# A weight sum of a Strassen pair as one vector instruction instead of two

## The chip, the cores and the metric

One Trainium2 chip, one core. The metric is device time in microseconds of one whole execution, all stages from the first load to the last store. The engines are called as in the profile: PE is the matrix engine and PEld its weight loads, DVE the vector engine, ACT the scalar engine, POOL the general-purpose engine, and SP the engine whose queue issues most of the DMAs.

## What is computed

A two-layer trunk for a prompt group of 512 tokens and a sample group of 8 tokens that share all weights. Everything is f32. In words, for each layer:

```python
h = rmsnorm(x, norm_g)
b_c, c_c, x_c, g_c, q, k, v, g_r = split(h @ w_in)        # w_in: 2048 x 8192
y_conv = b_c * conv3(c_c * x_c) * silu(g_c)               # causal, depthwise, width 3
y_ret = groupnorm(retention(rope(q), rope(k), v)) * gn_g * silu(g_r)
x = x + concat(y_conv, y_ret) @ w_out                     # 2048 x 2048
x = x + sigmoid(x @ w_pg) * (p[i] @ w_ple)                # 2048 x 2048, 256 x 2048
```

A last RMSNorm gives the outputs, and the convolution rows and retention states of both groups are outputs too.

## The kernel before

The 512 + 8 = 520 tokens lie along the free dimension, feature tiles of 128 along the partitions. An activation tile is 128x520, and it is used in two halves of 260 tokens, `LEFT` and `RIGHT`. A matmul multiplies a 128x128 weight tile with a 128x260 half.

Exactness comes from splitting each f32 operand into a rounded part `hi` and a remainder `lo` (both fp32r); `mm3` then does three matmuls, hi·hi, hi·lo and lo·hi, at lines 247, 248 and 249. So each weight tile, after its DMA, is rounded by ACT (line 229) and its remainder is formed by DVE (line 230) before PE can use it. `split_w` does both, for up to four K tiles (128x512) at once.

The large products take the output columns two tiles at a time; such a pair is one call of `pair`. If its row number `s` is 0, it is done directly (`plain`). Otherwise its first `s` K tiles go through one level of a Strassen scheme with seven products instead of eight (`strassen`), and the K tiles from `s` on are done directly at its end. With `q = s // 2`, a pair loads four weight blocks of `q` K tiles, `w11`, `w21`, `w22` and `w12`, and forms four weight sums in place with `add`. Most pairs have `s` of 14 or 16, so `q` is 7 or 8; one has `s` = 12 and three have `s` = 8. There are 84 pairs with `s` > 0 in the program.

```python
w11 = raws(src0, 0)
times(a, w11, k1, True, False)                 # product 1: no sum
w21, w22 = raws(src1, 0), raws(src1, q)
add(w11, w11, w21, SUB)
add(w21, w21, w22, ADD)
times(b, w21, t1, True, False)                 # product 2: after two sums
add(w21, w22, w11, SUB)
times(a, w21, t2, False, True)                 # product 3: after a third sum
w12 = raws(src0, q)
add(w21, w12, w21, SUB)
times(d, w12, ...); times(a, w11, t3, ...)     # products 4 and 5
times(b, w21, ...)                             # product 6: after the fourth sum
times(a, w22, t4, False, True)                 # product 7
```

`add` (its instruction is line 319), `times` and `raws` each cut their `q` K tiles into parts of at most `CHA`, `CHS` and `CHL` tiles, all four before. The raw weights lie in a ring of 32 K tiles (`raw_ring`), which is exactly four blocks of eight; the split weights lie in a ring of 60 K tiles (`split_ring`), where a part of four takes eight, four of `hi` and four of `lo`. A part of the split ring comes free when PE has read it.

The order on each engine isn't the order of the code. A scheduler with a model of the engines lays out the instructions of all engines when the program is built; sums and splits are raised in priority by `WPRIO`. Each engine then works strictly in the order that is written. The copies of PSUM banks, which PE waits for, are at line 307 on ACT and DVE.

The program goes through each layer in stages: the heads (q, k, v and gate of four retention heads), the convolution (16 pairs, `CONVS`), the output projection (`OUT_ROWS`) and the gate projection (`GATES`).

Of the kernel before, what the change touches and what calls it, by code (L numbers as in the profile page):

```python
# [29 lines left out]
NSLOT = 75  # L30
CH = 4
CHS = 4
CHA = 4
CHL = 4
CK = 256
BUSY = 10**9
# [155 lines left out]
def trunk_kernel(  # L192
# [40 lines left out]
    def chunks(a, b, most=CH):  # L233

        n = (b - a + most - 1) // most
        e = [a + (b - a) * i // n for i in range(n + 1)] if n else [a]
        return list(zip(e, e[1:]))
# [52 lines left out]
    def strassen(x, src0, src1, s, step=None):  # L290
# [24 lines left out]
        def add(out, x, y, op):  # L315
            for i, j in chunks(0, q, CHA):
                n = slice(P * i, P * j)
                with tc.high_priority(offset=WPRIO):
                    V.tensor_tensor(out[:, n], x[:, n], y[:, n], op)  # L319
# [1159 lines left out]
```

## Time and profile before

| | |
|---|---|
| median of 3 runs | 2168.1 us (2167.59 to 2169.01) |
| the profiled execution, first to last instruction (its span) | 2167.3 us |
| PE busy | 2147.8 us, 17861 matmuls |
| DVE busy | 1896.1 us, 3849 instructions |
| ACT busy | 1264.5 us, 2647 instructions |
| DMA | 387.31 MB, mean 179 GB/s |

The span is the profiled execution's own time; the median of the runs is 0.8 us above it. Busy is the time in which an engine has an instruction at work. An instruction's duration in the trace reaches to the end of its writes, and the next one on the same engine may start a little earlier, so durations of a group add up to more than its share of the busy time.

### The profile page before, as it was taken

To read this page: it belongs to the slowest core of one execution; us is meant where nothing else is said; L and a number is where in the kernel's file an instruction comes from. 1 tells how busy PE (TensorE), PEld (TensorE's weight loads), DVE (VectorE), ACT (ScalarE), POOL (GpSimd) and SP (SyncE) were. 2 spreads that over 40 slices of the span, in tenths; PEclk is the share of its full clock that TensorE was granted. 3 is DMA by queue.
4 is the path that set the end of the run, shared out by engine and by line. 5 is a ranking of instruction groups with operands and counts; after the bars stand their busy time and mean duration, and the time that the engine had idled before them with its cause. 6 is when DMAs were issued, how large, how long until landed. Compare 5 with 4: busy or idle time off the path is not lost. (4 is left out here: it accounts for less than half of the span.)

```text
span 2167.3 us, 48178 instructions
## 1 busy us (share of the span) xinstructions
PE 2147.8 (99%) x17861; PEld 2142.1 (99%) x17861; DVE 1896.1 (87%) x3849; ACT 1264.5 (58%) x2647; POOL 430.6 (20%) x746
## 2 busy tenths in 40 slices
PE   9999999999999999999999999999999999999998
PEld 9999999999999999999999999999999999999998
DVE  8889988998999987987997988989999998879884
ACT  8656655565555655655765655565645555456565
POOL 2313222211001211200212222231111022011011
PEclk9999999999999999999999999999999999999999
DMA  8555565545543745645645566664464355566455
GB/s 288 171 175 197 181 217 184 178 157 175 158 129 118 238 156 187 215 154 160 215 144 175 172 213 191 189 209 170 151 182 149 120 158 202 176 207 200 128 164 198
DMA packets 182861, 387.31 MB, mean 179 GB/s; under 512 B 25888, under 2 KB 56352, under 8 KB 182624
## 3 DMA queue, kind: packets, MB, share of 16 engines
q1 hardware_dynamic: 128704, 212.98, 31.6%
q0 software_dynamic: 53056, 169.84, 23.8%
q8 instruction: 140, 2.29, 0.4%
q10 hardware_dynamic: 864, 1.39, 0.2%
q14 instruction: 97, 0.79, 0.1%
HBM read 318.96 MB, written 65.15 MB: 177 GB/s over the span
## 5 line engine op out<-in xcount | busy, mean ns | idle before, releaser
L247 PE MATMUL ps_g<-slot,split 128*128 128x260 f32 x5465 | 1531.6, 284 | 7.2 <-ACT slot L307 2.9
L248 PE MATMUL ps_g<-slot,split 128*128 128x260 f32 x5465 | 1534.3, 282 | 0.3 <-DVE slot L555 0.3
L249 PE MATMUL ps_g<-slot,split 128*128 128x260 f32 x5461 | 1519.9, 283 | 0.5 <-DVE split L230 0.5
L229 ACT ACTIVATE split<-raw 128x512 fp32r<-128x512 f32 (+2 forms) x1347 | 777.3, 596 | 583.1 <-DVE raw L319 213.2
L247 PEld LDWEIGHTS ps_g<-slot,split 128*128 128x128 f32 x5465 | 1024.0, 188 | 10.1 <-ACT slot L307 3.7
L248 PEld LDWEIGHTS ps_g<-slot,split 128*128 128x128 f32 x5465 | 1028.5, 188 | 0.5 <-DVE slot L555 0.5
L249 PEld LDWEIGHTS ps_g<-slot,split 128*128 128x128 f32 x5461 | 1019.8, 188 | 1.0 <-DVE split L230 1.0
L230 DVE TENSOR_TENSOR split<-raw,split 128x512 fp32r<-128x512 f32 (+2 forms) x1346 | 849.2, 652 | 172.5 <-PE ps_g L248 85.4
L319 DVE TENSOR_TENSOR raw<-raw 128x512 f32<-128x512 f32 (+1 forms) x660 | 428.9, 660 | 32.5 <-DMA raw<-wi 23.7
L307 ACT ACTIVATE slot<-ps_g 128x260 f32<-128x260 f32 x336 | 127.4, 381 | 140.6 <-PE ps_g L249 122.7
L551 ACT ACTIVATE slot<-slot 128x520 fp32r<-128x520 f32 (+1 forms) x212 | 109.2, 562 | 46.6 <-DVE slot L414 11.1
L552 DVE TENSOR_TENSOR slot<-slot,slot 128x520 fp32r<-128x520 f32 (+1 forms) x212 | 124.4, 620 | 4.1 <-ACT slot L551 3.9
L781 POOL DMA_DIRECT2D o_rets<-slot x64 | 35.3, 552 | 351.6 <-DVE slot L780 131.7
L307 DVE TENSOR_TENSOR slot<-ps_g,slot 128x260 f32<-128x260 f32 x168 | 70.9, 424 | 6.0 <-PE ps_g L249 3.7
L869 POOL DMA_DIRECT2D slot<-hs x64 | 46.2, 724 | 118.7 <-DVE split L230 42.7
L814 POOL DMA_DIRECT2D hs<-slot x64 | 35.6, 556 | 139.3 <-DVE slot L755 61.3
L780 DVE SCALAR_TENSOR_TENSOR slot<-slot,vs,slot 128x256 f32<-128x256 f32 x128 | 56.1, 481 | 4.5 <-ACT slot L776 4.3
L746 DVE TENSOR_TENSOR slot<-slot,slot 128x520 f32<-128x520 f32 x80 | 55.8, 698 | 4.7 <-DMA o_rets<-slot 3.7
L770 POOL DMA_DIRECT2D slot<-sret x64 | 35.5, 554 | 114.6 <-ACT split L229 37.3
L1058 POOL DMA_DIRECT2D slot<-x1s x76 | 40.8, 538 | 87.6 <-PE ps_g L249 27.2
L1209 POOL DMA_DIRECT2D x2s<-slot x30 | 16.4, 545 | 201.6 <-DVE slot L1204 200.6
L771 POOL DMA_DIRECT2D slot<-kq x64 | 34.9, 547 | 106.0 <-DVE slot L876 22.2
(217 smaller groups left out, 1733.8 us busy)
## 6 DMA issues: line engine op xcount, KB each, us to landing
raw<-wi SPq DMA_DIRECT2D x377, 256.0 KB, 3.9
raw<-wo SPq DMA_DIRECT2D x128, 256.0 KB, 5.4
raw<-wg SPq DMA_DIRECT2D x122, 256.0 KB, 4.1
raw<-wi SPq DMA_DIRECT2D x136, 192.0 KB, 4.0
slot<-x1s POOLq DMA_DIRECT2D x76, 260.0 KB, 5.1
slot<-sret POOLq DMA_DIRECT2D x64, 256.0 KB, 4.0
hs<-slot POOLq DMA_DIRECT2D x64, 256.0 KB, 4.0
slot<-hs POOLq DMA_DIRECT2D x64, 256.0 KB, 5.2
```

Source lines behind the costliest of these rows:

```text
L229: S.activation(hi, raw, AF.Copy)
L230: V.tensor_tensor(lo, raw, F(hi), SUB)
L247: PE.matmul(out, wh, xh, start=start, stop=False, skip_group_check=more)
L248: PE.matmul(out, wh, xl, start=False, stop=False, skip_group_check=more)
L249: PE.matmul(out, wl, xh, start=False, stop=stop, skip_group_check=more)
L307: fn(*args)
L319: V.tensor_tensor(out[:, n], x[:, n], y[:, n], op)
L551: keep(S.activation(hi, src[:, n], AF.Copy))
L552: V.tensor_tensor(lo, src[:, n], F(hi), SUB)
L746: V.tensor_tensor(out[:, n], v, table[:, n], MUL)
L780: keep(V.scalar_tensor_tensor(st[:, c], k, vs[:, h, e, b : b + 1], st[:, c], MUL, ADD))
L869: SIDE.dma_start(t[:, :512].rearrange("p (m n) -> p m n", m=2), src)
```

## The change

```diff
-CHA = 4
+CHA = 8
```

`CHA` is used in one place:

```python
def add(out, x, y, op):
    for i, j in chunks(0, q, CHA):
        n = slice(P * i, P * j)
        with tc.high_priority(offset=WPRIO):
            V.tensor_tensor(out[:, n], x[:, n], y[:, n], op)
```

A sum over `q` = 8 K tiles was two DVE instructions of 128x512 and is one of 128x1024; for `q` = 7 it was 128x384 and 128x512 and is 128x896; for `q` = 6 it was two of 128x384 and is one of 128x768. The three pairs with `q` = 4 had one instruction a sum and keep it. That makes 336 sum instructions where there were 660. `times` still splits in parts of four K tiles, and the loads are still in parts of four.

The program holds the same instructions on PE, ACT, POOL and SP as before, but the scheduler lays them out anew. The next rows are DVE's, in the convolution of the second layer, before; names with `slot` are activation tiles, `raw` and `split` are the two weight rings, L319 are sums, L230 remainders.

```order
L319 TENSOR_TENSOR raw<-raw 128x512 x2
L307 TENSOR_TENSOR slot_1145_21830<-ps_g,slot_1145_21830 128x260
L746 TENSOR_TENSOR slot_1149_22061<-slot_1145_21830,slot_1048_19069 128x520
L230 TENSOR_TENSOR split<-raw,split 128x512
L319 TENSOR_TENSOR raw<-raw 128x512
L230 TENSOR_TENSOR split<-raw,split 128x512
L307 TENSOR_TENSOR slot_1146_21831<-ps_g,slot_1146_21831 128x260
L780 SCALAR_TENSOR_TENSOR slot_1142_21759<-slot_1143_21760,vs,slot_1142_21759 128x256 x2
L319 TENSOR_TENSOR raw<-raw 128x512 x2
```

The last L230 of these rows is the first part of product 2. Only three half sums stand ahead of it: the first half of both sums, and the second half of the first sum. The same place with the change:

```order
L307 TENSOR_TENSOR slot_1145_21574<-ps_g,slot_1145_21574 128x260
L746 TENSOR_TENSOR slot_1149_21801<-slot_1145_21574,slot_1048_18853 128x520
L230 TENSOR_TENSOR split<-raw,split 128x512
L319 TENSOR_TENSOR raw<-raw 128x1024
L307 TENSOR_TENSOR slot_1146_21575<-ps_g,slot_1146_21575 128x260
L780 SCALAR_TENSOR_TENSOR slot_1142_21503<-slot_1143_21504,vs,slot_1142_21503 128x256 x2
L319 TENSOR_TENSOR raw<-raw 128x1024
L784 ISA slot_1143_21504,osum<-slot_1142_21503,slot_1143_21504 128x256
L784 ISA osum 128x1
L230 TENSOR_TENSOR split<-raw,split 128x512
L784 ISA slot_1143_21504,osum<-slot_1142_21503,slot_1143_21504 128x256
L784 ISA osum 128x1
L230 TENSOR_TENSOR split<-raw,split 128x512 x3
```

Both whole sums now stand ahead of product 2's first part, which is the first of the three at the end, and so do the retention updates L780 and L784 and one other remainder, which stood behind it or elsewhere.

PE's order at the same place, before. Product 2 of this pair reads `slot_741`, `slot_757`, `slot_769` and so on; product 7 of the pair before it reads `slot_743`, `slot_759`, `slot_771`.

```order
L247 MATMUL ps_g<-slot_811_14204,split 128x260
L248 MATMUL ps_g<-slot_811_14204,split 128x260
L249 MATMUL ps_g<-slot_811_14204,split 128x260
L249 MATMUL ps_g<-slot_741_13732,split 128x260
L247 MATMUL ps_g<-slot_757_13845,split 128x260
L248 MATMUL ps_g<-slot_758_13846,split 128x260
L249 MATMUL ps_g<-slot_757_13845,split 128x260
```

And with the change:

```order
L247 MATMUL ps_g<-slot_811_14048,split 128x260
L248 MATMUL ps_g<-slot_811_14048,split 128x260
L249 MATMUL ps_g<-slot_811_14048,split 128x260
L247 MATMUL ps_g<-slot_743_13580,split 128x260
L248 MATMUL ps_g<-slot_744_13581,split 128x260
L249 MATMUL ps_g<-slot_743_13580,split 128x260
L247 MATMUL ps_g<-slot_759_13693,split 128x260
L248 MATMUL ps_g<-slot_760_13694,split 128x260
L249 MATMUL ps_g<-slot_759_13693,split 128x260
```

Product 7 of the pair before is put in front: the L249 on `slot_741`, the first matmul that needs the remainder of product 2, stands 24 places further back in PE's whole order. All in all 7979 of the program's 17827 matmuls have another place, half of these by at most 9 places and nine in ten by at most 24; the rest keep theirs.

## Rows read from the trace of the kernel before

**Rows 1.** The page: span and busy time of the engines.
```profile
span 2167.3 us, 48178 instructions
...
PE 2147.8 (99%) x17861; PEld 2142.1 (99%) x17861; DVE 1896.1 (87%) x3849; ACT 1264.5 (58%) x2647; POOL 430.6 (20%) x746
```

**Rows 2.** Groups by line and shape: busy us, mean ns, idle before.
```profile
L247 PE MATMUL ps_g<-slot,split 128*128 128x260 f32 x5437 | 1523.6, 284 | 7.2 <-ACT slot L307 2.9 <-ACT ps_g L307 1.6 <-ACT split L229 1.5
...
L319 DVE TENSOR_TENSOR raw<-raw 128x512 f32<-128x512 f32 x520 | 354.1, 688 | 17.6 <-DMA raw<-wi 12.1 <-DMA raw<-wo 2.9
...
L319 DVE TENSOR_TENSOR raw<-raw 128x384 f32<-128x384 f32 x140 | 77.4, 554 | 14.9 <-DMA raw<-wi 11.6 <-DMA raw<-wg 2.8
```

**Rows 3.** Busy us by stage: stretch, length, PE, PEld, DVE, ACT, POOL; then clock, DMA.
```profile
530.00:704.00 174.00, 174.00 (x1454) 174.00 (x1454) 158.71 (x312) 93.58 (x188) 18.33 (x24) 1.00 0.44 134
704.00:1112.00 408.00, 404.68 (x3368) 403.57 (x3367) 353.44 (x683) 247.63 (x501) 73.83 (x133) 1.00 0.58 186
...
1612.00:1786.00 174.00, 173.57 (x1443) 172.74 (x1442) 161.32 (x321) 95.14 (x200) 20.17 (x28) 1.00 0.46 142
1786.00:2145.00 359.00, 356.48 (x2963) 355.60 (x2961) 291.45 (x542) 208.47 (x428) 60.32 (x113) 1.00 0.56 183
sum 2075.00, PE 2066.72 PEld 2062.95 DVE 1828.62 ACT 1206.04 POOL 409.89; mean PE 344.45 PEld 343.82 DVE 304.77 ACT 201.01 POOL 68.31
```

**Rows 4.** What PE waited for, whole span: us in total, times, longest.
```profile
PE ps_g L247 <- ACT slot L307: 2.9, 4, 1.3
PE ps_g L247 <- ACT ps_g L307: 1.6, 2, 1.2
PE ps_g L247 <- ACT split L229: 1.5, 2, 1.3
...
PE ps_g L249 <- DVE split L230: 0.5, 1, 0.5
```

**Rows 5.** What the splits waited for, whole span: us in total, times, longest.
```profile
ACT split L229 <- DVE raw L319: 213.2, 160, 4.3
...
ACT split L229 <- PE ps_g L249: 186.2, 220, 3.9
...
DVE split L230 <- PE ps_g L248: 85.4, 109, 2.2
```

**Rows 6.** The same waits in the second convolution stage, 1612 to 1786 us.
```profile
ACT split L229 <- DVE raw L319: 30.6, 21, 4.3
...
DVE split L230 <- PE ps_g L248: 0.8, 1, 0.8
```

**Rows 7.** Timeline, 1683 to 1692 us: start, us to the last one's end, instruction.
```profile
1683.16 1.41 DVE L319 TENSOR_TENSOR raw<-raw 128x512 f32<-128x512 f32 x2
1684.49 0.42 DVE L307 TENSOR_TENSOR slot<-ps_g,slot 128x260 f32<-128x260 f32 x1
...
1685.56 0.68 DVE L230 TENSOR_TENSOR split<-raw,split 128x512 fp32r<-128x512 f32 x1
1686.28 0.69 DVE L319 TENSOR_TENSOR raw<-raw 128x512 f32<-128x512 f32 x1
1686.89 0.69 DVE L230 TENSOR_TENSOR split<-raw,split 128x512 fp32r<-128x512 f32 x1
1687.49 0.42 DVE L307 TENSOR_TENSOR slot<-ps_g,slot 128x260 f32<-128x260 f32 x1
1687.83 0.87 DVE L780 SCALAR_TENSOR_TENSOR slot<-slot,vs,slot 128x256 f32<-128x256 f32 x2
...
1687.92 0.40 PE L249 MATMUL ps_g<-slot,split 128*128 128x260 f32 x2
...
1688.62 1.29 DVE L319 TENSOR_TENSOR raw<-raw 128x512 f32<-128x512 f32 x2
1689.82 0.42 DVE L784 CUSTOM_DVE_ANT_0 slot<-slot,slot 128x256 f32<-128x256 f32 x1
...
1690.17 0.69 DVE L230 TENSOR_TENSOR split<-raw,split 128x512 fp32r<-128x512 f32 x1
```

## The prediction, on record before the changed kernel ran

> **What bounds the kernel now.** Look first at the page's busy times [rows 1]. PE has work in 2147.8 of 2167.3 us, so it is idle for 19.5 us. DVE, the engine that the change touches, is busy 87% of the span, which is high but isn't the bound by itself. Does a busy PE run at its pace, or does waiting hide between its matmuls? The stage table answers that [rows 3]: from 530 to 704 us PE is never idle and starts 1454 matmuls in 174 us, one each 0.120 us; from 1612 to 1786 us it is 1443 in 173.57 us, one each 0.120 us again. The pace is one number, and DVE's load doesn't move it. So the time is the number of matmuls times a fixed pace, plus PE's idle time. The change leaves the number of matmuls as it is. It can act through PE's idle time alone.
>
> Where is that? The sum row of the stage table covers 70 to 2145 us: 2075 us less 2066.72 us busy is 8.3 us; the other 11.2 us lie in the start and the tail. Of the 8.3 us, the stretch from 704 us has 3.3 and the one from 1786 us has 2.5 [rows 3]. These two begin an output projection, whose first pair has `s` = 0 and forms no weight sums. What is left for all stages whose pairs are fed by sums is about 2.4 us.
>
> Then the list of what PE waited for [rows 4]. Most of it is for PSUM copies on ACT (2.9 and 1.6 us); for a rounded part it waited 1.5 us in two places, for a remainder 0.5 us once. PE never waits for a sum itself, but a sum stands ahead of each split, and the last list shows it there [rows 5]: ACT, about to round, waited for a sum 160 times, 213.2 us in all. That is ACT's time, not the kernel's. As against that, ACT waited 186.2 us and DVE 85.4 us for PE to free a piece of the split ring, 329 times in all. A split that waits for the ring is as far ahead of PE as the ring is long: 60 K tiles hold 7.5 parts of four, and each part feeds 12 matmuls, so 7.5 x 12 x 0.120 = 10.8 us at most. In most of the program, then, the splits run well ahead of PE.
>
> The exception is the convolution. There DVE is busy 158.71 of 174 us and 161.32 of 174 us, 91 and 93% [rows 3]; in the second of these stages DVE waited for the ring only once, 0.8 us, and ACT waited 21 times for a sum [rows 6]. The lead is used up there. The timeline shows how far [rows 7]: the first remainder of a product 2 ends at 1686.89 + 0.69 = 1687.58 us. In PE's order its first matmul is the second of two L249 in a row; those two start at 1687.92 us, 0.12 us apart, so it starts at 1688.04 us. The lead is 0.46 us.
>
> **The change, part by part.** *Removed:* 660 - 336 = 324 sum instructions. The columns to be added stay the same, so what goes is the fixed part of an instruction. The means of the two sizes [rows 2] give the slope: 688 - 554 = 134 ns for 128 columns, so 536 ns for 512. Back to back, a 128x512 instruction takes 0.61 us from start to start (the sum at 1686.28, the remainder at 1686.89) and one of 0.60 follows (1686.89 to 1687.49) [rows 7]. Its fixed part is 0.60 - 0.536 = 0.065 us or a little more. So DVE gets back 324 x 0.065 = 21 us of its 1896, about 1%, spread over the program; in each convolution stage with 16 pairs it is 16 x 4 x 0.065 = 4 us over the stage and its edges. Where the lead is 10 us, that buys nothing, since PE's pace hides it. In the convolution it lets the splits regain lead. What it can give is bounded below by 0 and above by the 2.4 us of idle time worked out above. I take 0.4 us, near the one wait for a remainder [rows 4], since the others are for ACT.
>
> The Trainium skill (Perfetto Trace Analysis, Optimizing Scalar/DVE Operations) gives some 60 ns of overhead for a DVE instruction on SBUF and says that larger operations help where the engine is saturated. By its figure the gain on DVE is an estimated 324 x 60 ns = 19 us, much as by the rows. The same section speaks against the change too: where DVE isn't saturated but causes bubbles elsewhere, it advises to break instructions up. Here DVE is the first in the convolution alone.
>
> *Added:* the first part of a product must wait for the whole sum. A 128x1024 sum lasts about 688 + 536 = 1224 ns where the first half lasted 688, so products 3 and 6 can start 0.54 us later and product 2, behind two sums, 1.07 us. The second part is ready no later than before. Also, a sum that follows another one on the same block has to see it end; before, the halves could alternate. The two sums at 1683.16 us show the price, 1.33 us to the next start instead of 1.20 [rows 7]; 0.13 us of DVE at one or two places in each of 81 pairs is 10 to 20 us, so DVE's net gain lies between about 0 and 21 us. What hides the delay is the lead. If it hid nothing, the price would be 81 x (1.07 + 0.54 + 0.54) = 174 us; at a lead of several us it is 0.
>
> *Moved:* the scheduler has laid out the order with the longer sums in mind. Follow the tight place through the new order, with the times of [rows 7]. The two half sums that took 1683.16 to 1684.49 are no longer ahead of L307, so the remainder that started at 1685.56 can start 1.33 us earlier, at 1684.23 (if nothing else holds it). Then come 0.60 for it, 1.14 for the first whole sum, 0.34 for L307, 0.79 for the two L780, 1.14 for the second sum, 0.35 for L784, 0.60 for another remainder and 0.35 for the second L784: 1689.54. Product 2's first remainder ends 0.69 later, at 1690.23 us, 2.65 us later than before. But PE's order has 24 matmuls of the former pair's product 7 in front of it now, 24 x 0.120 = 2.88 us: it is wanted at 1690.92 us, and the lead is 0.7 us, where it was 0.46. So the new order pays for the delay at the tightest place. The step works as long as the scheduler's durations are true; at three places of before PE did wait for a split [rows 4], which shows by how much it errs: 0.5 to 1.3 us. I take two more such waits of about 0.5 us, +1.0 us; none if the order is as good everywhere as here, about 10 us if every second of the some 40 tight sums of the two convolution stages costs 0.54 us.
>
> *The sum:* 2167.3 - 0.4 + 1.0 = 2167.9 us for a profiled execution. The median of the runs lies 0.8 us above the profiled one, so 2168.7 us. A difference of under 0.2%, or 4.3 us, is about what a measurement of this kernel can't tell from no change.
>
> **The rivals.** *PE's idle time grows (slower).* ACT works in order. When a rounding waits 0.54 to 1.07 us longer for a whole sum, the PSUM copies that stand behind it on ACT come later, and PE already waits for those most [rows 4]. For it: 160 waits of ACT for sums, 37 or so of them where the lead is short [rows 5, 6]. Against it: the place followed above, and that ACT is idle 42% of the time. It decides from the point where the lead falls below 0.54 us at more than eight products: 8 x 0.54 = 4.3 us. If all the some 40 tight sums cost half a microsecond, it is 20 us; I take 8 of them beyond the forecast's two, +5.4 us in all: about 2173 us.
>
> *The relief of DVE counts (faster).* If the 21 us were wholly kept and DVE's load in the convolution were what starves ACT, the 2.4 us of idle time in those stages would go, and the looser DVE would also shorten the starts of the output projections, where PSUM copies wait in a crowd of splits. For it: DVE at 91 to 93%. Against it: no more than 8.3 us can go from 70 to 2145 us, and more than half of it stands in stretches without sums. All of it gone is 2168.1 - 8.3 = 2159.8 us; half is 2164.
>
> *The order decides, not the sums.* Nearly half of the matmuls have another place, so the few idle stretches are drawn anew, also where no sum stands. Of 8.3 us, half may go or half as much again come: 2164 to 2172 us. It is of the size of what can't be told, and either sign is as likely.
>
> **How the numbers follow.** No change that can be told: 0.60, the forecast and most of the redrawn orders. Slower: 0.25, the longer waits on ACT or an unlucky order, since a bad order has no upper bound and a good one gains 8.3 us at most. Faster: 0.15. The likeliest case's own range is 2164 to 2172 us. The whole range reaches down to 2163, over half of the idle time gone, and up to 2177, where 16 or so sums cost 0.54 us each.
>
> **What the profile would show.** If the steps are right: 336 instructions at L319, those of 128x1024 near 1224 ns, DVE's busy time lower by up to 21 us, PE's idle time from 70 to 2145 us still 5 to 12 us, and its pace 0.120 us. If the waits on ACT take over, ACT's wait for L319 grows well over 213 us and PE's waits for L307 or L229 over 6 us. If the relief counts, PE's idle time falls below 4 us. The prediction is wrong if a stall over 2 us appears at a sum or if DVE's load in the convolution turns out to have held PE by way of ACT.

## The result, and the profile of the changed kernel

The changed kernel takes 2187.4 us (median of 4 runs, 2186.4 to 2190.5), the kernel before on the same chip 2168.6 us. The ratio is 1.0093, with a 95% interval of 1.0078 to 1.0107: 18.8 us slower, where the prediction said no change (2168.7 us) and its range ended at 2177.

The page of the changed kernel, against [rows 1] and [rows 2]:

```profile
span 2185.5 us, 47393 instructions
...
PE 2156.0 (99%) x17861; PEld 2146.8 (98%) x17861; DVE 1880.4 (86%) x3525; ACT 1248.6 (57%) x2647; POOL 433.5 (20%) x746
...
L319 DVE TENSOR_TENSOR raw<-raw 128x1024 f32<-128x1024 f32 (+2 forms) x336 | 384.4, 1144 | 32.2 <-DMA raw<-wi 25.2
```

The 336 sums are there, and DVE is busy 15.7 us less. PE is idle 29.5 us of its span, where it was 19.5; its busy time has grown by 8.2 us with the same matmuls. The table by stretch of time, against [rows 3], tells where (the same view, and the same columns):

```profile
70.00:530.00 460.00, 458.66 (x3829) 458.01 (x3829) 411.39 (x820) 269.96 (x588) 119.02 (x203) 1.00 0.57 185
530.00:704.00 174.00, 172.71 (x1426) 171.18 (x1426) 155.50 (x272) 88.73 (x182) 17.40 (x22) 1.00 0.41 132
704.00:1112.00 408.00, 403.26 (x3348) 402.65 (x3348) 347.19 (x629) 243.34 (x498) 74.09 (x135) 1.00 0.57 187
1112.00:1612.00 500.00, 493.69 (x4095) 491.23 (x4094) 436.18 (x860) 281.30 (x627) 119.56 (x200) 1.00 0.56 178
1612.00:1786.00 174.00, 172.90 (x1433) 171.82 (x1432) 156.54 (x274) 89.31 (x183) 17.33 (x21) 1.00 0.42 134
1786.00:2145.00 359.00, 355.08 (x2943) 354.46 (x2943) 295.45 (x512) 202.49 (x424) 61.13 (x114) 1.00 0.56 186
```

Read the counts of matmuls in brackets rather than the busy time. A matmul's bar is 283 ns long (mean) and the next starts 120 ns after it, so a late start of up to 0.16 us leaves no gap between the bars, and a longer one shows 0.16 us less than it lost. The count in a fixed stretch has no such blind spot. In the two stretches that the prediction calls the convolution it fell from 1454 + 1443 to 1426 + 1433: 38 matmuls, 4.6 us at 0.120 us each, where the busy time admits 2.0 us. Matching each instruction with its place in the program shows that these stretches hold only the later half of each convolution: in the kernel before, its 16 pairs run from about 380 to 720 us and from about 1438 to 1790 us. The stretch from 1112 to 1612 us, with the heads of the second layer and the first half of its convolution, lost most. Its row of the kernel before was not among those shown:

```profile
1112.00:1612.00 500.00, 498.93 (x4168) 498.22 (x4168) 446.66 (x959) 289.99 (x633) 119.05 (x203) 1.00 0.58 182
```

That is 73 matmuls, 8.8 us, 59 of them ahead of 1438 us, in the heads; the two stretches with the projections lost 20 each, 4.8 us together, the first stretch the 7 that are left.

What PE waited for, against [rows 4], and what the splits waited for, against [rows 5], over the whole span:

```profile
PE ps_g L247 <- ACT slot L307: 7.9, 10, 2.3
PE ps_vt L913 <- DMA slot<-hs: 2.7, 2, 1.9
PE ps_g L249 <- DVE split L230: 2.3, 6, 0.6
PE ps_g L247 <- ACT ps_g L307: 2.2, 2, 1.2
...
ACT split L229 <- DVE raw L319: 189.0, 101, 5.1
ACT split L229 <- PE ps_g L249: 166.9, 133, 7.0
...
DVE split L230 <- ACT split L229: 105.2, 134, 4.7
```

PE waits longer for PSUM copies on ACT (L307) and six times for a remainder, where it was once. ACT's own wait for sums has not grown (213.2 before), though one such wait is now 1.9 us long on the mean, where it was 1.3. DVE's remainders wait 105.2 us for ACT's roundings, where it was 69.3.

What whole sums wait for can be seen on DVE at the place that the prediction walked through, the pair of [rows 7], some 13 us later in this run:

```profile
1695.42 1.29 DVE L230 TENSOR_TENSOR split<-raw,split 128x512 fp32r<-128x512 f32 x2 [0.30 <-ACT split L229]
1697.34 0.43 DVE L307 TENSOR_TENSOR slot<-ps_g,slot 128x260 f32<-128x260 f32 x1 [0.62 <-PE ps_g L249]
...
1698.72 0.69 DVE L230 TENSOR_TENSOR split<-raw,split 128x512 fp32r<-128x512 f32 x1 [0.22 <-PE ps_g L248]
1699.45 1.23 DVE L319 TENSOR_TENSOR raw<-raw 128x1024 f32<-128x1024 f32 x1
1700.59 0.42 DVE L307 TENSOR_TENSOR slot<-ps_g,slot 128x260 f32<-128x260 f32 x1
1700.93 0.87 DVE L780 SCALAR_TENSOR_TENSOR slot<-slot,vs,slot 128x256 f32<-128x256 f32 x2
1701.72 1.22 DVE L319 TENSOR_TENSOR raw<-raw 128x1024 f32<-128x1024 f32 x1
...
1705.23 1.29 DVE L230 TENSOR_TENSOR split<-raw,split 128x512 fp32r<-128x512 f32 x2 [1.01 <-ACT split L229]
```

The second L230 of the row at 1695.42 is product 1's first remainder, the L230 at 1698.72 its second. This one waited for PE to free a piece of the split ring. Then come the two whole sums, and at 1705.23 product 2's first remainder. Sum 1 overwrites `w11`, the block that product 1 is split from, so a whole sum 1 can't begin until *both* parts of product 1 have been split, and the second part has to wait for the ring. In [rows 7] the first halves of sums 1 and 2 run at 1683.16, ahead of product 1's second remainder at 1685.56: they don't need product 1's second part. From the end of product 1's second remainder to the end of product 2's first one it was 1.34 us (1686.24 to 1687.58), and is 6.51 us now (1699.41 to 1705.92). Not all of that is the sums: ahead of this remainder DVE waits 1.01 us for ACT, which has the part's rounding in the row at 1704.58, behind that of product 5's first part, which waited for PE until 1701.66:

```profile
1701.66 0.63 ACT L229 ACTIVATE split<-raw 128x512 fp32r<-128x512 f32 x1 [5.23 <-PE ps_g L249]
...
1704.58 1.66 ACT L229 ACTIVATE split<-raw 128x512 fp32r<-128x512 f32 x3
```

Counted over the program by matching each instruction with its place in the order: before, the first half of sum 1 began ahead of product 1's last remainder in 74 of the 84 pairs, that of sum 3 (which overwrites product 2's block) ahead of product 2's in 72 of the 81 with two halves, that of sum 4 ahead of product 3's in 75 of 81; in the changed kernel none does. The median time between the two remainders went from 2.75 to 5.68 us at product 2 and from 1.54 to 4.88 us at product 3. The lead (end of a product's first remainder to the start of the first matmul that reads it, median) fell from 5.7 to 3.8 us at product 2 and from 5.4 to 2.8 us at product 3.

### The profile page after: what moved, and what is told of

The parts are those of the page before. It is cut to its first block, busy times and chain, and to the rows that moved or that the text cites. A ratio compares the mean times of both kernels' runs of the same rounds, so it can differ in the third digit from the quotient of the medians.

```text
span 2185.5 us, 47393 instructions
## 1 busy us (share of the span) xinstructions
PE 2156.0 (99%) x17861; PEld 2146.8 (98%) x17861; DVE 1880.4 (86%) x3525; ACT 1248.6 (57%) x2647; POOL 433.5 (20%) x746
## 4 chain that ended last, share of the span: by engine, by line
PE 86%; DVE 4%; DMA 3%; issue 3%; ACT 3%; POOL 0%; SPq 0%; DVEq 0%; POOLq 0%; ACTq 0%
PE ps_g L247 27%; PE ps_g L249 27%; PE ps_g L248 27%; DVE split L230 1%; ACT split L229 1%; DMA raw<-wi 1%; DVE raw L319 1%; ACT slot L551 1%; DMA slot<-ys 1%; PE ps_p L247 0%; PE ps_p L249 0%; PE ps_p L248 0%; DMA slot<-hs 0%; DMA o_rets<-slot 0%; PE ps_vt L913 0%
## 5 line engine op out<-in xcount | busy, mean ns | idle before, releaser
L249 PE MATMUL ps_g<-slot,split 128*128 128x260 f32 x5461 | 1517.1, 283 | 2.5 <-DVE split L230 2.3
L229 ACT ACTIVATE split<-raw 128x512 fp32r<-128x512 f32 (+2 forms) x1347 | 754.0, 594 | 589.4 <-DVE raw L319 189.0
L249 PEld LDWEIGHTS ps_g<-slot,split 128*128 128x128 f32 x5461 | 1019.4, 189 | 4.2 <-DVE split L230 4.2
L230 DVE TENSOR_TENSOR split<-raw,split 128x512 fp32r<-128x512 f32 (+2 forms) x1346 | 832.6, 647 | 190.5 <-ACT split L229 105.2
L319 DVE TENSOR_TENSOR raw<-raw 128x1024 f32<-128x1024 f32 (+2 forms) x336 | 384.4, 1144 | 32.2 <-DMA raw<-wi 25.2
L307 ACT ACTIVATE slot<-ps_g 128x260 f32<-128x260 f32 x336 | 126.8, 381 | 176.7 <-PE ps_g L249 153.2
L307 DVE TENSOR_TENSOR slot<-ps_g,slot 128x260 f32<-128x260 f32 x168 | 70.7, 421 | 13.6 <-PE ps_g L249 12.7
L780 DVE SCALAR_TENSOR_TENSOR slot<-slot,vs,slot 128x256 f32<-128x256 f32 x128 | 55.8, 477 | 8.2 <-ACT slot L776 6.9
```

The lines of the kernel that those rows point to most:

```text
L229: S.activation(hi, raw, AF.Copy)
L230: V.tensor_tensor(lo, raw, F(hi), SUB)
L249: PE.matmul(out, wl, xh, start=False, stop=stop, skip_group_check=more)
L307: fn(*args)
L780: keep(V.scalar_tensor_tensor(st[:, c], k, vs[:, h, e, b : b + 1], st[:, c], MUL, ADD))
```

## The experiments

Each kernel is compared with the kernel before on the same chip. One table first; the accounts below refer to it. "Conv" is the number of matmuls at work in the two stretches of the later convolution (530 to 704 and 1612 to 1786 us; 2907 is the most that any kernel reached, both stretches without a gap). The stretches are fixed in time, so a late kernel is still at earlier work in the second one: the matmul that starts it in the kernel before comes 15 us later in the changed kernel, some 35 us in e7 and e17, 118 us in e2, and their counts compare only roughly. "Lead" is that of products 2 and 3, worked out as above. In e5 and e6 the sums named are whole, the others halves.

| kernel | sums | us | ratio, 95% interval | conv | lead, us |
|---|---|---|---|---|---|
| before | halves | 2168.6 | | 2897 | 5.7, 5.4 |
| changed | whole | 2187.4 | 1.0078–1.0107 | 2859 | 3.8, 2.8 |
| e1 changed order | halves | 2186.9 | 1.0059–1.0100 | 2867 | 4.2, 2.8 |
| e2 order of before | whole | 2315.3 | 1.0652–1.0709 | 2510 | 3.9, 3.9 |
| e3 other order | halves | 2174.1 | 1.0012–1.0037 | 2901 | 6.0, 5.4 |
| e4 other order | whole | 2193.9 | 1.0102–1.0137 | 2859 | 3.8, 2.7 |
| e5 sums 1 and 2 | whole | 2191.7 | 1.0091–1.0120 | 2884 | 3.5, 2.9 |
| e6 sum 4 | whole | 2176.6 | 1.0023–1.0050 | 2901 | 6.0, 5.2 |
| e7 five raw blocks | whole | 2216.0 | 1.0204–1.0238 | 2790 | 2.7, 2.6 |
| e8 five raw blocks | halves | 2183.8 | 1.0055–1.0090 | 2875 | 5.4, 4.2 |
| e9 held | halves | 2179.8 | 1.0036–1.0061 | 2879 | 4.4, 3.4 |
| e10 as e7, own block | whole | 2175.6 | 1.0019–1.0042 | 2907 | 6.9, 5.6 |
| e11 as e8, own block | halves | 2177.0 | 1.0025–1.0050 | 2907 | 6.9, 6.6 |
| e12 | parts of two | 2183.2 | 1.0053–1.0081 | 2895 | 5.9, 4.7 |
| e13 first part waits | halves | 2185.1 | 1.0068–1.0101 | 2884 | 4.3, 3.0 |
| e14 own block, ring of four | whole | 2182.5 | 1.0046–1.0083 | 2907 | 7.0, 5.4 |
| e15 own block, ring of four | halves | 2171.2 | 1.0004–1.0021 | 2907 | 7.7, 6.7 |
| e16 split ring of 56 | halves | 2192.6 | 1.0099–1.0134 | 2886 | 4.9, 4.3 |
| e17 split ring of 56 | whole | 2219.6 | 1.0213–1.0242 | 2787 | 2.6, 2.5 |
| e18 as e14, other order | whole | 2184.6 | 1.0049–1.0082 | 2907 | 6.8, 5.2 |

**The instruction or the order (e1, e2).** Both write out the order of every engine by hand. e1 takes the changed kernel's order and puts two half sums, side by side, where a whole one stands; e2 takes the order of before for all but the sums and makes 298 of the 324 pairs of halves whole (the other 26 would wait for work that stands behind them in that order).

```diff
-CHA = 8
+CHA = 4
...
+        for a, b in zip(row, row[1:]):
+            tc.add_manual_dep(b, a.name, edge, reason="order")
```

> Sums in halves again (660 instructions), but every engine keeps the order of the changed kernel, the two halves of a sum side by side where the whole sum stood. Theory A, the new order costs the time: 2187 us, 2183 to 2191, PE idle again near 29 us with the long stalls at the same places. Theory B, the coarse sum itself costs it (a first part that waits for a whole sum): the first part can start 0.54 us earlier again, so most of the loss goes, 2168 to 2174 us. Theory C, DVE's load: 21 us more on DVE than in the changed kernel, so slower than it, over 2190 us.

> The order of the kernel before on every engine for all instructions but the sums; 298 of the 324 sums are whole, 26 that cannot be whole in that order stay in halves. Theory A, the new order costs the time: no loss, 2164 to 2172 us. Theory B, the coarse sum itself costs it: 298 of 324 parts of the loss or more, since nothing makes up for the delay of 0.54 to 1.07 us now, 2180 to 2200 us.

e1 is as slow as the changed kernel, as theory A had it, though DVE has 14 us more work from 70 to 2145 us (the sum rows of the changed kernel and of e1):

```profile
sum 2075.00, PE 2056.30 PEld 2049.34 DVE 1802.26 ACT 1175.13 POOL 408.52; mean PE 342.72 PEld 341.56 DVE 300.38 ACT 195.85 POOL 68.09
sum 2075.00, PE 2054.49 PEld 2048.50 DVE 1816.31 ACT 1184.21 POOL 409.39; mean PE 342.42 PEld 341.42 DVE 302.72 ACT 197.37 POOL 68.23
```

In that order the size of the sums, and DVE's fixed time, are worth nothing: what costs is how the work is laid out for whole sums. e2 shows why it had to be laid out anew. In the order of before, whole sums cost 147 us, far beyond what either theory expected (2200 us at most):

```profile
ACT split L229 <- DVE raw L319: 499.9, 193, 6.8
...
PE ps_g L247 <- ACT ps_g L307: 37.7, 21, 4.4
PE ps_g L247 <- ACT slot L307: 23.8, 22, 3.9
PE ps_g L247 <- ACT split L229: 21.5, 19, 2.7
```

ACT waits 500 us for sums (213.2 before), and behind it in its queue the PSUM copies come late for PE. The new order recovers all but 19 of the 147 us.

**Other orders (e3, e4).** The priority of sums and splits is raised, with halves (e3) and whole sums (e4).

```diff
-WPRIO = 20
+WPRIO = 400
```

> The kernel before with one number changed that only orders: the priority of sums and splits 400 steps ahead instead of 20. 4158 matmuls get another place; the sums stay in halves. Theory A in its widest form (any new order costs some 10 to 20 us): 2178 to 2190 us. Theory B: within 5 us of the kernel before, 2163 to 2173 us.

> The changed kernel, sums whole, with the same priority of 400: 3054 matmuls get another place against the changed kernel. Theory A (it is the one order that is unlucky): anywhere from 2164 to 2190 us, and not where the changed kernel is. Theory B (the coarse sum costs it whatever the order): 2183 to 2192 us.

Whole sums cost 19.7 us here, 18.8 in the first pair, so it isn't one unlucky order. But e3 is itself 6 us slower than before at the median, a microsecond above what B allowed, and e4 two above. Its runs spread from 2168.0 to 2179.7 us, and the profiled one is the fastest of them, as fast as the kernel before: that its convolution and leads are untouched doesn't tell what the slower ones lost.

**Which sum (e5, e6).** `add` gets its part size as an argument.

```diff
-        add(w11, w11, w21, SUB)
-        add(w21, w21, w22, ADD)
+        add(w11, w11, w21, SUB, 8)
+        add(w21, w21, w22, ADD, 8)
```

> Only the two sums ahead of product 2 are whole (162 of the 324), the other two in halves; the scheduler orders anew. If the delay of product 2, which stands behind two whole sums, is what costs the time: most of the 19 us, 2181 to 2190 us. If each whole sum costs alike, half of it: 2175 to 2180 us. If any new order costs it: near 2187 us too, as the fourth sum alone would then do.

> Only the sum ahead of product 6 is whole (81 of the 324); products 4 and 5, which need no new sum, stand between it and its use. 5910 matmuls get another place. If delay is the cause, this sum has the most time in hand: 2164 to 2171 us, no loss. If each whole sum costs alike: 2172 to 2174 us. If any new order costs it: 2180 to 2190 us.

The first two sums alone bring all of the changed kernel's loss, and 4 us more. The fourth alone (`add(w21, w12, w21, SUB, 8)` in e6) leaves the leads of products 2 and 3 and the convolution as before and is 8 us slower, a figure that none of the three theories had. It does shorten the lead of the product that it feeds: product 6's fell from 5.2 to 4.2 us, and sum 4 begins ahead of product 3's last remainder in none of 81 pairs (75 before). How much of the 8 us that is, and how much single stalls at the starts of stages, is not shown.

**A fifth raw block (e7, e8).** The raw ring has 40 tiles instead of 32; to make room the split ring has 56 instead of 60.

```diff
-RAW = 32
+RAW = 40
...
-SPLIT = 60
+SPLIT = 56
```

> The changed kernel with a ring of five raw blocks instead of four (RAW 40), paid for by a split ring of 56 K tiles instead of 60. Theory R: the four raw blocks close a loop, a later sum frees its block later, so the next load and the next pair's sums come later still, and a fifth block opens the loop: within 6 us of the next kernel, the same with sums in halves. Theory D, only the delay between a sum and its product counts: 15 to 25 us slower than the next kernel.

> The kernel before with the ring of five raw blocks and the split ring of 56: the partner of the kernel ahead of it. Theory R: the loads come earlier and the leads grow, 2155 to 2168 us. Theory D: nothing to gain beyond a new order, 2163 to 2176 us.

The theory that the raw ring's length makes whole sums late fell: with five blocks they cost more, 32 us, not less. (The shorter split ring has a part in this: with it and four raw blocks they cost 27 us, e16 and e17 below.) D's figures (15 to 25 us, and 2176 us at most for e8) were passed too.

**Held halves, and a late first part (e9, e13).** e9 has halves and forbids any half sum to be issued ahead of the former product's last remainder. e13 has halves and lets the rounding of a first part wait for both halves of its sum. The hold of e9 (`LAST` is the remainder issued last):

```diff
-                    V.tensor_tensor(out[:, n], x[:, n], y[:, n], op)
+                    s = V.tensor_tensor(out[:, n], x[:, n], y[:, n], op)
+                    tc.add_manual_dep(s.ins, LAST[0], mybir.DependencyInfo(mybir.DependencyClass.NoSync, mybir.DependencyReason.DATA), reason="held")
```

> The kernel before with its sums in halves and one thing added: no half of a sum may start on DVE before the previous product's last remainder has been issued there. Each half is still 688 ns long and the DVE work is that of before. Theory W (the cost of the change is that a whole in-place sum waits until both parts of its block have been split, so the sums no longer run beside the splits of the product ahead): this alone gives the changed kernel's time, 2183 to 2195 us, and no sum starts ahead of that remainder. Theory D (the cost is the length of a whole sum, 0.54 to 1.07 us more before a first part): 2168 to 2174 us, as the kernel before.

> The kernel before with its sums in halves, and one thing added: the first part's rounding of products 2, 3 and 6 waits for the second half of the sum too. The halves may still run beside the splits of the product ahead, so this is the delay of a product's first part alone (the term that the prediction priced), without the serialization. e9 had the serialization without this delay and lost 10.8 us of the changed kernel's 18.8. If the rest is this delay: 2173 to 2180 us, some 5 to 10 us above before. If the delay costs nothing, as the prediction took it: 2166 to 2172 us. If it is the whole cost after all: 2183 us or more, which with e9 would mean that the two don't add.

Neither theory got its figure for e9; W missed by 3 us, D by 6. The hold alone, with DVE's work as before, costs 10.8 us and shortens the leads by 1.3 and 2.0 us. e13 costs 16.4 us, more than the rest that e9 left. It isn't the delay alone, though: its order has sums 3 and 4 begin ahead of the former product's last remainder in 1 of 81 pairs each (sum 1 in 66 of 84), so the scheduler gave most of the overlap up by itself. That the two shares don't add up to more than the whole is seen; how they divide is not settled.

**The first sum in a block of its own (e10, e11, e14, e15, e18).** The first sum writes to a free raw block, so it no longer overwrites what product 1 is split from. e10 and e11 do it with the rings of e7 and e8, e14 and e15 with those of before: there the free block is the one that `w12` will be loaded into, and `w12` takes the block that becomes free.

```diff
-        add(w11, w11, w21, SUB)
+        s1 = raw_ring.get(q)
+        add(s1, w11, w21, SUB)
+        raw_ring.put(w11)
+        w11 = s1
```

> Whole sums, a raw ring of five blocks and a split ring of 56 as in e7 (2216 us), with one thing changed: the first sum is written to a fifth block of its own, so it does not wait for product 1 to have been split; the third and fourth sums are still in place. Theory W: a good part of the 32 us between e7 and e8 goes, 2185 to 2205 us, since e5 put the whole cost on the first two sums. Theory D (length of the sums): 2212 to 2220 us, as e7. If the fifth block's load is what counts (it comes free only when the pair's sums are done), both this and e11 are slower than e7 and e8.

> The partner of e10 with sums in halves: the price of whole sums, once the first needs no block that is still being split, is the difference of e10 and this. Theory W: this stays near e8 (2180 to 2190 us), as halves waited for little, and e10 is less than 20 us above it (32 us in e7 and e8). Theory D: e10 stays some 30 us above it.

> The changed kernel with whole sums, raw ring of four blocks and split ring of 60 as it is, and one thing changed: the first sum is written to the raw block that is free at that time, and w12 is loaded later into the block that this frees. Theory W (waiting for the splits of the product ahead, through the first sum above all): most of the 19 us goes, 2168 to 2178 us. Against it stands that w12's load has less time: if that is what counts, 2185 us or more, with waits of sums for the load. If DVE's 21 us were worth anything once nothing waits: below 2167 us.

> The partner of e14 with sums in halves. Theory W: within 5 us of e14, as e10 and e11 were within 1.4 us of each other. If it is above e14 by more than 4 us, whole sums are worth something for DVE; if it is below e14 by 10 us or more, the length of a whole sum costs time by itself.

> Whole sums and the first sum in the free raw block as in e14, in another order: the priority of sums and splits raised from 20 to 400, as in e3 (halves in place, 2174.1 us) and e4 (whole in place, 2193.85 us). Theory W: most of the 19.7 us between e3 and e4 goes, 2170 to 2184 us, and the two convolution stages have no idle time of PE, as in e10, e11, e14 and e15. Theory O or the length of a whole sum: near e4, 2188 us or more.

From e7 to e10 one thing is changed, and 40 us go, 9 more than W hoped for at best; e10 is no slower than its partner with halves (which is 3 us faster than W had it). The two convolution stretches of e7 and then of e10:

```profile
530.00:704.00 174.00, 170.80 (x1386) 168.61 (x1387) 149.80 (x265) 87.59 (x180) 17.27 (x21) 0.99 0.42 129
1612.00:1786.00 174.00, 171.05 (x1404) 168.65 (x1404) 152.24 (x268) 88.31 (x180) 21.86 (x25) 1.00 0.45 142
```

```profile
530.00:704.00 174.00, 174.00 (x1454) 174.00 (x1453) 159.35 (x279) 95.35 (x189) 18.51 (x24) 1.00 0.44 132
1612.00:1786.00 174.00, 174.00 (x1453) 174.00 (x1452) 159.26 (x282) 99.07 (x203) 19.80 (x27) 1.00 0.45 137
```

PE has no gap left in either stretch, and so it is in all five of these kernels, whole or halves, in both orders. Sum 1 begins ahead of product 1's last remainder in 83 or 84 of 84 pairs. But in the changed kernel's own rings this buys only 5 us (e14), and 9 us in the other order (e18, against e4). e14 missed what W expected by 4.5 us, e18 by half a microsecond, though leads and convolution came out as W has them. What e14 still loses lies in a few long stalls in the heads and the projections, by its profiled execution, which is the slowest of six (2176.9 to 2189.3 us). The second longest, 3.1 us from 259.5 us on, ends behind this sum and the remainder that follows it:

```profile
257.02 0.20 DVE L984 BATCH_NORM_AGGREGATE mv<-st 128x2 f32<-128x6 f32 x2
260.01 1.09 DVE L319 TENSOR_TENSOR raw<-raw 128x896 f32<-128x896 f32 x1 [2.78 <-DMA raw<-wi]
```

A whole sum (sum 2 of its pair) at the head of DVE's queue waits for a load, and the splits behind it wait too. e15, with halves, has no such stall; it is 11 us faster than e14 and the best of the eighteen, 2.5 us above before. That went against W, which had the two within 5 us: by the mark set there, the size of the sums still costs time when the first one waits for no split. Whether it is a whole sum's length, its wait for loads, or sums 3 and 4, which are still in place, is open. In e14 sums 3 and 4 never begin ahead of the former product's last remainder, in e15 they do in 56 and 61 of 81 pairs; in e10 and e11 it is the same (none, and 42 and 48), at no cost.

**A shorter split ring (e16, e17).** `SPLIT` is 56, all else as before, with halves and whole sums.

> The kernel before, sums in halves, raw ring of four, and only the split ring cut from 60 to 56 K tiles. It tells what the shorter split ring is worth in e7, e8, e10 and e11: 2174 to 2184 us if it is the reason that e8, e10 and e11 are above before; 2166 to 2171 us if the redrawn order and the fifth block are.

> The partner of e16 (2192.6 us, halves) with whole sums in place, split ring 56, raw ring of four. Theory W (a whole sum in place waits for the splits of the product ahead): 10 to 35 us above e16, 2203 to 2228 us, as in the three other pairs that differ in the sums alone and have the first sum in place (18.8, 19.7 and 32 us). Theory O (what counts is that the order is another than that of the kernel before, and the size of the sums doesn't matter): within 10 us of e16 on either side.

Four tiles less cost 24 us with halves, more than expected, so the shorter ring is enough to explain that e8 is slower than before (e16, without the fifth block, is slower still). Whole sums cost 27 us more: a fourth pair in which sums in place cost 19 to 32 us.

**Smaller sums (e12).** `CHA` is 2, splits stay in parts of four.

> The change in the other direction: sums in parts of two K tiles, so about 650 more sum instructions of 128x256 than before, at 0.065 us of fixed part each some +42 us of DVE's busy time (1896 to near 1938 us). Theory W: a sum in smaller parts follows the splits more closely, and DVE's time is hidden where the lead is long: 2166 to 2180 us. If DVE's busy time were worth its length where DVE is 91 to 93 per cent busy (40 of the 320 us of the change's kind, two convolution stages), 10 us or more above before with PE's new waits in those stages for remainders.

DVE is busy 1936.8 us, 41 more than before; the two stretches lose two matmuls and the time grows by 14 us, 3 us more than W allowed. So neither finer nor coarser sums than before help here.

## Why the prediction was wrong

*The bound held in the main.* PE's pace between stalls is 0.120 us as before, with the same matmuls. But "it can act through PE's idle time alone" was too narrow: of the 18.2 us of the span 10.0 are idle time and 8.2 busy time. Some 4.6 of these lie in three spells at half the granted clock (last section), for which the prediction had no term; the others are late starts that the bars hide.

*Removed.* DVE's busy time fell by 15.7 us, not 21 (0.048 us a sum instead of 0.065). That it buys nothing was right: e1 has 14 us more DVE work from 70 to 2145 us than the changed kernel, in the same order, and the same time.

*Added: the step that failed.* The prediction priced a longer instruction: products 3 and 6 0.54 us later, product 2 1.07 us, "the second part is ready no later than before". A whole sum lasts 1.23 us, as it said. What it left out is that the sums work in place. A whole sum waits until the product ahead has split both of its parts, the second of which waits for the split ring; a half waited for the first part alone. Measured over the program, product 2's first remainder comes 2.9 us later behind product 1's last one and product 3's 3.3 us later behind product 2's (medians), about three and six times the priced delay; at the place above, part of it is ACT's order. The rows to see it in were at hand: in [rows 7] two sums run ahead of the remainder at 1685.56. Four pairs that differ in the sums alone, each with its order laid out anew, show +18.8, +19.7, +32 and +27 us with the first sum in place; of the two pairs with a block of its own, one shows −1.4, the other +11.3. That the wait costs time is shown by e7 and e10 (40 us for the first sum's place); in the changed kernel's own rings that sum's place is worth 5 us, and sums in halves as well another 11 (e14, e15).

*Moved.* The hand walk began with "the remainder that started at 1685.56 can start 1.33 us earlier, at 1684.23 (if nothing else holds it)". In the changed kernel it was held: it waited 0.22 us for PE to free a piece of the ring, behind an L307 that had waited 0.62 us for PE. The walk had 6.0 us from its start to the end of product 2's first remainder, the trace has 7.2, and the lead at this place became 0.09 us, not 0.7 (0.46 before). From this one place the prediction concluded that the new order pays for the delay everywhere. The new order does pay for most: in the order of before whole sums cost 147 us (e2), and 19 are left. That the prediction's bound of 174 us is near to 147 is chance, as it priced the length of the sums alone.

*The sum's +1.0 us* was the term that should have held this. The 18.2 us of the span split up as follows: 4.6 us in the two convolution stretches (6.3 if the same matmuls are followed by their place in PE's order, since the second stretch comes 15 us later here); some 4.6 us in the three spells of a lower clock; the rest, 7 to 9 us, in single stalls in the second layer's heads, at the starts of the output projections and elsewhere.

*The rivals.* The one that ended on the slower side named the right place of the loss: PE's waits for L307 and L229 went from 6.0 us to over 10. Its mechanism was only half right. ACT did not wait longer for sums in all (189 us), and its price of 0.54 us for each tight sum was too small. "The order decides" held either sign as likely; of the seventeen experiments with another order (all but e2) none is faster than before, and all but e15 are slower by more than 0.2%. But most of them also change something that costs time by itself: whole sums, a hold, the shorter split ring. Only e3 changes the order alone, with a median 6 us above before and a fastest run that equals it. That an order which leaves 8 us of idle time in 2075 has little to gain and much to lose from being drawn anew is argued, with e3 for it, not shown. The relief of DVE never counted.

The Trainium skill (Perfetto Trace Analysis, Optimizing Scalar/DVE Operations), which the prediction weighed, advises to break instructions up where an engine isn't saturated but causes bubbles elsewhere. The step from whole sums to halves agrees with it in four pairs, 19 to 32 us; the step from halves to parts of two (e12, 14 us slower) does not.

*Open.* How the 18.8 us divide between the lost overlap, the later first part (e9 and e13 bring 10.8 and 16.4 us and don't add) and waits for loads, and why each of the single stalls outside the convolution stands where it does. They have different last waits (a PSUM copy, a load, a remainder), move with each order, and remain with the first sum out of place (e14, e18). No kernel here beats the one before.

## What to carry to other kernels

Before making an in-place operation coarser, ask who still reads the block that it overwrites: the coarse one waits for the last reader of the whole block, the fine one for the reader of its part, and that can cost more than the instruction's own length (2.9 and 3.3 us here, for one of 1.23). Writing the result to a block that is free at the time removes the wait, but pays only as far as the loads then still come in time (40 us in one ring here, 5 in another). Where the engine that bounds the time is idle for only 0.4% between start and tail, don't take a redrawn order for neutral: the one kernel here that changes nothing else took 0 to 12 us more. And judge stages by how many matmuls they start, not by busy time, in stretches that hold the same work.

## What the runs showed of the hardware

Three times in the changed kernel the granted clock fell to half, 1.2 GHz of the two levels, for 3.41 us each (from 731.2, 1355.9 and 1813.2 us), each time just behind one of the three longest stalls of PE (2.2 to 2.7 us from start to start). The same table around the second, before the stall, with the stall, and after it:

```profile
1349.00:1352.00 3.00, 3.00 (x28) 3.00 (x27) 3.00 (x7) 1.41 (x3) 1.31 (x3) 1.00 0.77 199
1352.00:1355.90 3.90, 1.98 (x17) 1.77 (x16) 3.90 (x10) 2.62 (x6) 1.75 (x3) 1.00 0.83 230
1355.90:1359.30 3.40, 3.40 (x17) 3.40 (x17) 1.12 (x3) 1.19 (x3) 0.54 (x1) 0.50 0.98 298
1359.30:1362.70 3.40, 3.40 (x31) 3.40 (x30) 1.64 (x2) 1.63 (x3) 0.00 (x0) 1.00 0.95 351
```

At 0.50, PE starts 16 matmuls in 3.4 us (the row's 17 counts one already at work) where 28 are usual: some 1.5 us lost each time, 4.6 in all, though PE counts as busy throughout. So such a stall can cost more than half as much again as it lasts. It does not always: in e15 a stall of 2.1 us from 743.5 us on is followed by no such spell, nor is one of 2.8 us in e8 from 730.6 us on. e2, with stalls up to 4.7 us, has 14 such spells, some 25 of its 147 us. In the kernel before, the longest stall between start and tail was 1.6 us, and no such spell stands there.
